# An mLSTM, GLA and SSD decoder trunk on one core: the mLSTM's row operations begin at the second GLA value, and other steps of the lanes are moved

## Chip, core and metric

One core of a Trainium2 chip runs the whole program in one launch. The metric is the device time of one execution in microseconds (us), given as the median of several runs. A profile is one further execution, recorded instruction by instruction. The engines are named as the profile names them: PE (TensorE, matrix products; PEld are its weight loads), DVE (VectorE), ACT (ScalarE), POOL (GpSimd) and SP (SyncE, which issues most transfers).

## What is computed

The reference is one step of a two-layer decoder trunk on 512 prompt tokens and 8 x 4 sample tokens, 544 tokens in all, with 1024 features, in 32-bit floats.

```python
def _trunk(x, ...):
    for l in range(DEPTH):
        if l % 2 == 0:
            mix, c, n, m, s = _ab_mixer(x, ...)
        else:
            mix, h, cv = _ssd_mixer(x, ...)
        x = _layernorm(DN_ALPHA * x + mix, ...)
        x = _layernorm(DN_ALPHA * x + _mlp(x, ...), ...)
```

The AB mixer of layer 0 has two groups of four heads, mLSTM and GLA, fed by one input projection, and one output projection behind both. The mLSTM's part that matters here is its row arithmetic, on one row of 544 numbers for each of four heads: a log-sigmoid, a running sum `b`, a running maximum, and exponentials of their differences.

```python
    lf = jax.nn.log_sigmoid(mf + fg_bias)
    b = jnp.cumsum(lf, axis=1)
    g = b + m0
    D = b[t] - b[s] + ig[s]          # for s <= t
    m = jnp.maximum(g, D.max(axis=2))
    w_intra, w_inter = jnp.exp(D - m), jnp.exp(g - m)
    h = num / jnp.maximum(jnp.abs(den), jnp.exp(-m))
```

GLA multiplies each score by the exponential of a difference of decays, feature by feature, which the kernel does level by level (1, 2, 4, ... 256 tokens). Layer 1 is a Mamba-2 SSD mixer. Behind each mixer stand a layer normalisation, a squared-ReLU MLP of 4096 features, and another normalisation.

## The kernel before

**Products.** Features lie on the 128 partitions and tokens in two halves of 272 columns. A 32-bit product is made of three products of rounded parts (hi by hi, hi by lo, lo by hi), so an output block of 128 features over 1024 input features is 8 x 3 = 24 matmuls for each half, 48 for both (`dense`, L378). This text calls one such matmul *a product*. Weights come by DMA; ACT makes the rounded part `whi` (L167) and DVE the rest `wlo` (L168).

**Order.** PE's order is written out by hand: within the AB, output projection, MLP and SSD stages PE runs exactly what the program lists, in that order. The order of DVE, ACT and POOL is not written out: a planner at compile time sorts their instructions by readiness and by the place at which they are listed. `issue_after` adds an edge: what is listed inside it stands behind a given instruction on that engine.

**Lanes.** All small work (scores, transposes, normalisations) is written as generators, the *lanes*. `tick()` is called ahead of every product and moves each lane by one; `yield n` lets n further ticks pass, so what follows stands n + 1 products later in PE's order. `W` (L36) holds those numbers by name. `need(key)` polls once a tick until another lane has set the key; it costs no instruction. `until` and `flush` drive lanes on without products.

**The AB stage** runs 20 blocks (GLA's q, k and v, the mLSTM's q, k and v, and GLA's gate gg), 960 products, then four tail blocks (the mLSTM's output gate mo), the first half of all four and then the second, 192 products. Between the halves, at product 1056, `until("mheads")` forces the mLSTM's heads to an end; `take_place` then closes the pool with the score tiles and lists four loads of the residual `xf` on POOL (L325). The lanes in it:

- `gla_lane`: `gla_decay` (steps `dec`), then for each of two feature blocks `gla_scores`: the diagonal `gd` after `s0` products for the first block and `sc` for the second; nine levels (`gs`), `lev` apart, each with a difference F on POOL (L1085), two exponentials on ACT (L1087, L1088), and zq and zk on DVE (L1092, L1094); then a transpose `kdt` after `kd`. Then the sample scores (`ss`), the final state (`end`), and `gla_samples` and `ml_samples`, each with `c0` ahead of its values, `u` ahead of each of six outer products `supd` (L1008, with a masked copy `vm` on POOL, L1004) and `s` ahead of the last transpose.
- `gla_heads`: for each head the value `num` (L869), on whose emission the key ("g", h) is set; its normalisation ends in four instructions on ACT that write `hn` (L897); `out` products later a transpose `hot` (L903), and after `hd` the next head. The keys ("gT", q) hold heads 0 and 1, then 2 and 3, back until the scores of block q are there.
- `ml_lane`: `ml_gates` lists the row arithmetic in three blocks, each inside `hold("head")`, which puts it behind the last DVE and ACT instruction of the GLA value listed last. The first block is L1226 to L1237, and stands behind `need("gscores")`, a key that `gla_lane` sets when the scores of both feature blocks are there; in the same tick, just before it, value 2 is listed. The second (L1241 to L1254) and third (from L1258) need ("g", 2). After ("g", 3), `gates` products on, PE transposes the rows (`uwt`, L1280), and `gr` and again `gr` later come small matmuls `sc` (L1288 to L1293). Then `pipeline` runs the four heads of the mLSTM in steps `mr` products apart, with up to four heads at different points in one step: transpose, scores (`md`, `mo`), value, and a broadcast row (`rowbc`). `ml`, a wait within a head's generator, has no effect there: `pipeline` takes no notice of it.
- `tokmajor` (lane "v", steps `v`): transposes of v.

PSUM tiles of this stage come from `pm`, which takes a fifth tile of its own on each fifth call and otherwise goes round four.

**Normalisations** (`layernorm`) are two steps per half, sum and variance: `l0` and `v0` for the first half, `l1` and `v1` for the second, `ls` and `vs` instead for the second half ahead of MLP 1. The last one (`last_layernorm`) has `f0`, `f1` and `f2`. In SSD, `sg` stands ahead of each group's first step.

Of the kernel before, what the change touches and what calls it, by code (L numbers as in the profile page):

```python
# [32 lines left out]
HEADM = 6  # L33
HEADA = 2

W = dict(dec=12, gates=30, gr=8, sc=16, lev=16, v=24, kd=10, out=48, hd=6, s0=42, ss=40, end=12, c0=20, u=13, s=16, ml=12, mr=52, dt=238, sg=72, sx=14, sq=26, so=48, l0=12, l1=12, v0=74, v1=55, f0=16, f1=18, f2=4, ls=20, vs=47)  # L36
GATES = ((0, 0, 4), (32, 4, 4), (64, 8, 16))
LEVELS = (64, 32, 16, 8, 4, 2, 1)

# [189 lines left out]
def trunk_kernel(ctx, tc, a, stages=("ab", "mlp0", "ssd", "mlp1")):  # L229
# [8 lines left out]
    def pm(name):  # L238
        turn[0] += 1
        k = spare[0] and turn[0] % 5 == 0  # L240
        return psm.tile([P, 512], F32, tag="k" if k else "m", name=name, bufs=1 if k else 4)
# [91 lines left out]
    def need(*keys):  # L333
        while not ready.issuperset(keys):
            yield 0
# [114 lines left out]
    def layernorm(hf, i, pool, out=None):  # L450
# [4 lines left out]
        which = norms_done[0] - hf  # L455
        yield W["l0" if not hf else "ls" if i == 2 else "l1"]
        mu = pm("mu")
# [8 lines left out]
        V.tensor_tensor(q[:, 0], q[:, 0], q[:, 1], ALU.add)  # L466
        yield W["v0" if not hf else "vs" if i == 2 else "v1"]
        var = pm("var")
# [34 lines left out]
    def last_layernorm(i, pool, out):  # L503
# [6 lines left out]
        def less(mu, k, f):  # L510
            V.scalar_tensor_tensor(x[:, k:k + 2], mu[:, None, :n].broadcast_to([P, 2, n]), f, x[:, k:k + 2], ALU.mult, ALU.add)
        yield W["f0"]
        mu = pm("mu")
# [9 lines left out]
        for k in range(h, KT - 1):  # L523
# [4 lines left out]
            V.tensor_tensor(q[:, 0], q[:, 0], q[:, k], ALU.add)  # L528
        yield W["f1"]
        mu, var, rp = pm("mu"), pm("var"), pm("rp")  # L530
        TE.matmul(mu[:, :n], ones, s, start=True, stop=False)
        yield W["f2"]
        TE.matmul(var[:, :n], ones, q[:, 0], start=True, stop=False)
# [182 lines left out]
    def ab(pool, early, then):  # L716
# [67 lines left out]
        def tokmajor(key, h):  # L784

            x = fm[key + "v", h]
            if h == 0:
                vt[key] = pool.tile([P, 4, 4, 130], F32, tag="vt", name="vt", bufs=2)
                G.memset(vt[key][:, :, :, 128:], 1.0)
                vraw[key] = pool.tile([P, 4, NS], F32, tag="vs", name="vs", bufs=1)  # L790
            yield W["v"]
            p = pm("vtr")
# [337 lines left out]
        def hold(what="last", mx=None):  # L1130

            st = ExitStack()
            for x in (mx or gla)[what]:
                st.enter_context(tc.issue_after(x))
            return st
# [79 lines left out]
        ml = {}  # L1215

        def ml_gates():
            rw = early.tile([P, T], F32, name="rw", bufs=1)
            uw = early.tile([P, T], F32, name="uw", bufs=1)
            z, t, b, u = rw[0:4], rw[32:36], rw[64:68], uw[0:4]  # L1220
            G.memset(uw, 0.0)
            S.copy(z, gate[32:36])
            S.copy(u, gate[0:4])
            yield from need("gscores")
            with hold("head"):
                S.activation(t, z, AF.Abs)  # L1226
                S.activation(t, t, AF.Exp, scale=-1.0)
# [173 lines left out]
        def ml_lane():  # L1401
            ml["cg"] = []
            yield from need(("gate", 0))
            yield from ml_gates()
            yield from need("gla", ("mq", 1), ("mk", 1))
            rows_bc(ml["nM"][:, :NP])
            ready.add("mscores")
            yield from pipeline([ml_head(h) for h in range(4)], W["mr"], (3, 1, 2, 0))
            ready.add("mheads")
            yield from ml_last()  # L1410
            ready.add("ml")
# [531 lines left out]
    while n < len(stages):  # L1943
        st = stages[n]
        src = spill
        with ExitStack() as stk:
            if st == "ssd":
# [5 lines left out]
                with tc.tile_pool(name="ssd", bufs=1, reuse_waits="tile") as pool:  # L1953
# [4 lines left out]
                    with tc.manual_schedule(engines={mybir.EngineType.PE}):  # L1958
                        out = ssd(pool, ypool, dram, right, ahead, consts)
# [174 lines left out]
```

## Time and profile before

| | us |
|---|---|
| median of 3 runs | 1504.7 |
| lowest and highest | 1504.12, 1508.48 |
| profiled execution, device time | 1502.27 |
| its span, first to last instruction | 1500.6 |

The prediction shows the profile's lines. In the page and the tables of stretches, each engine's busy time is in us, with the number of instructions behind x; PEclk is the clock granted to TensorE, as a share of full speed or, in the row of 40 digits, in tenths. A line of a timeline has the start in us from the first instruction, the duration, the engine, the line of the kernel, the operation, output <- inputs, sizes, the number of instructions merged, and in brackets the idle time of the engine ahead of it with what ended that. A matmul's duration is its latency; successive matmuls overlap, so it is their starts that show the rate.

### The profile page before, as it was taken

The numbers are of one execution on the slowest core, as the hardware profiler recorded it, in microseconds if no ns is written. First come the engines' busy times: TensorE is split into PE (matmuls) and PEld (weight loads), VectorE is DVE, ScalarE is ACT, GpSimd is POOL, SyncE is SP. The second block draws the span as 40 slices with busy tenths as digits, with TensorE's granted clock in tenths as the row PEclk, the third lists the DMA queues.
The fourth block names the chain that finished last, engine by engine and source line by source line (L and its number), as shares of the span: only waits on it lengthen the run. The fifth ranks groups of instructions, "written<-read, shape, count | busy, mean of one in ns | idle before, by whom it ended". The sixth has DMA issues, their size and how long they took to land.

```text
span 1500.6 us, 29204 instructions
## 1 busy us (share of the span) xinstructions
PE 1468.2 (98%) x11607; PEld 1419.1 (95%) x11607; DVE 1100.2 (73%) x2075; ACT 795.0 (53%) x1750; POOL 192.8 (13%) x228
## 2 busy tenths in 40 slices
PE   9998989999999999999999999999999999999997
PEld 8988989999999999999888789989999999999996
DVE  5675576786777667668999988777678677676656
ACT  7454457474444534537776675555247354444343
POOL 1410222100000000010243441421010000000000
PEclk9998999999999999999999999999999999999998
DMA  7211333413232332416657766365222333233221
GB/s 252 71 57 43 88 120 90 126 43 114 72 113 90 94 99 85 146 48 202 141 144 257 235 191 226 99 205 151 71 75 67 99 100 96 88 99 92 63 86 60
DMA packets 95025, 172.51 MB, mean 115 GB/s; under 512 B 15880, under 2 KB 50968, under 8 KB 94632
## 3 DMA queue, kind: packets, MB, share of 16 engines
q1 hardware_dynamic: 62280, 140.44, 30.3%
q10 hardware_dynamic: 29216, 17.19, 4.4%
q0 software_dynamic: 3392, 13.00, 2.3%
q8 instruction: 91, 1.49, 0.4%
q14 instruction: 46, 0.38, 0.1%
HBM read 153.48 MB, written 17.13 MB: 114 GB/s over the span
## 4 chain that ended last, share of the span: by engine, by line
PE 44%; DVE 5%; DMA 1%; issue 1%; ACT 1%; SPq 0%; DVEq 0%
PE psd L378 30%; PE psd L590 9%; PE yp L1712 1%; DVE wlo L168 1%; DVE acc L1606 1%; PE it L1759 1%; PE sp L1690 1%; PE ip L1687 1%; PE sps L1766 1%; DMA wraw<-mlp_w 0%; DVE h0n L1772 0%; PE xt L1651 0%; DMA ec<-d_ecs 0%; DVE xf L552 0%; DVE Y L1715 0%
## 5 line engine op out<-in xcount | busy, mean ns | idle before, releaser
L378 PE MATMUL psd<-xh,whi 128*128 128x272 f32 x1488 | 441.3, 297 | 1.0 <-ACT xh L287 1.0
L378 PE MATMUL psd<-xl,whi 128*128 128x272 f32 x1488 | 435.5, 293 | 1.3 <-DVE xl L478 1.3
L378 PE MATMUL psd<-xh,wlo 128*128 128x272 f32 x1488 | 435.7, 293 | 0.0
L378 PEld LDWEIGHTS psd<-xl,whi 128*128 128x128 f32 x1488 | 281.8, 190 | 7.9 <-issue 4.0
L378 PEld LDWEIGHTS psd<-xh,whi 128*128 128x128 f32 x1488 | 281.4, 189 | 8.0 <-issue 4.7
L378 PE MATMUL psd<-hh,whi 128*128 128x272 f32 x992 | 286.9, 289 | 0.0
L378 PE MATMUL psd<-hlo,whi 128*128 128x272 f32 x992 | 286.5, 289 | 0.0
L378 PE MATMUL psd<-hh,wlo 128*128 128x272 f32 x992 | 286.4, 289 | 0.0
L378 PEld LDWEIGHTS psd<-xh,wlo 128*128 128x128 f32 x1488 | 281.6, 189 | 4.4 <-issue 3.5
L168 DVE TENSOR_TENSOR wlo<-wraw,whi 128x1024 fp32r<-128x1024 f32 (+2 forms) x175 | 206.6, 1184 | 54.3 <-ACT whi L167 52.8
L167 ACT CAST whi<-wraw 128x1024 fp32r<-128x1024 f32 (+2 forms) x175 | 173.5, 997 | 130.2 <-PE psd L378 108.6
L378 PEld LDWEIGHTS psd<-hlo,whi 128*128 128x128 f32 x992 | 186.9, 188 | 0.2
L378 PEld LDWEIGHTS psd<-hh,whi 128*128 128x128 f32 x992 | 186.9, 188 | 0.2
L378 PEld LDWEIGHTS psd<-hh,wlo 128*128 128x128 f32 x992 | 186.9, 188 | 0.1
L428 DVE TENSOR_TENSOR xf<-xf,psd 128x272 f32<-128x272 f32 x208 | 88.4, 434 | 74.7 <-PE psd L378 74.2
L590 PE MATMUL psd<-xh,wlo 128*128 128x272 f32 x416 | 120.0, 289 | 0.0
L590 PE MATMUL psd<-xh,whi 128*128 128x272 f32 x416 | 119.9, 288 | 0.0
L590 PE MATMUL psd<-xl,whi 128*128 128x272 f32 x416 | 119.7, 288 | 0.0
L203 ACT CAST whi<-wsum 128x1024 fp32r<-128x1024 f32 x52 | 54.3, 1044 | 111.3 <-PE psd L590 70.2
L203 ACT CAST whi<-wraw 128x1024 fp32r<-128x1024 f32 (+1 forms) x52 | 43.4, 834 | 95.3 <-PE psd L378 84.2
L204 DVE TENSOR_TENSOR wlo<-wsum,whi 128x1024 fp32r<-128x1024 f32 x52 | 63.7, 1225 | 23.2 <-ACT whi L203 23.2
L590 PEld LDWEIGHTS psd<-xl,whi 128*128 128x128 f32 x416 | 78.5, 189 | 0.0
(488 smaller groups left out, 2836.4 us busy)
## 6 DMA issues: line engine op xcount, KB each, us to landing
wraw<-mlp_w SPq DMA_DIRECT2D x80, 512.0 KB, 3.7
wraw<-ssd_in SPq DMA_DIRECT2D x40, 512.0 KB, 3.8
wraw<-mlp_w SPq DMA_DIRECT2D x64, 256.0 KB, 3.0
wraw<-ab_in SPq DMA_DIRECT2D x22, 512.0 KB, 3.7
h<-h SPq DMA_DIRECT2D x32, 256.0 KB, 4.7
h0n<-h0n SPq DMA_DIRECT2D x16, 512.0 KB, 5.0
E<-d_cs ACTq DMA_DIRECT2D x16, 512.0 KB, 5.0
s_h<-h0n POOLq DMA_DIRECT2D x16, 512.0 KB, 4.0
```

Of the source, the lines that this page charges most:

```text
L167: nc.scalar.copy(hi[:, r], w[:, r])
L168: nc.vector.tensor_tensor(lo[:, r], w[:, r], hi[:, r].bitcast(F32), ALU.subtract)
L203: self.cut[0] = nc.scalar.copy(hi, x).ins
L204: self.cut[1] = nc.vector.tensor_tensor(lo, x, hi.bitcast(F32), ALU.subtract).ins
L378: last[0] = TE.matmul(ps[:, :TH], (hi, hi, lo)[t][:, k, :], (rh, rl, rh)[t], start=i == 0, stop=i == n - 1).ins
L428: V.tensor_tensor(x, x, ps, ALU.add)
L590: last[0] = TE.matmul(ps, wt[:, k], bt[:, k], start=first and n == 0, stop=n == 11, skip_group_check=not first).ins
L1606: V.scalar_tensor_tensor(acc[:, :n], ci[:, w:w + n], cw[:, m, w:w + 1], acc[:, :n], ALU.mult, ALU.add)
L1687: TE.matmul(ip[:, j * P:(j + 1) * P], hT[:, j * P:(j + 1) * P], Cf[:, tk], start=True, stop=True)
L1690: TE.matmul(sp, Bt[:, b], xw, start=True, stop=True)
L1712: TE.matmul(ypv[64 * e:64 * e + 64, j], z[:, 64 * r:64 * r + 64], E[:, r], start=True, stop=True)
L1759: TE.matmul(it[64 + NS * k:64 + NS * k + NS], Cm[:, NS * (q + k):NS * (q + k) + NS], h0[k], start=q == 0, stop=q == NB - 2)
```

## The change

The first block of the row arithmetic is held behind the key ("g", 1), the second GLA value (they are counted from 0), in place of "gscores". And 22 of the 31 numbers in `W` change: `mr` 52 to 62 (the mLSTM's heads), `s0` 42 to 36 (the first GLA level), and smaller moves of other lanes. No instruction is added or taken out.

```diff
-W = dict(dec=12, gates=30, gr=8, sc=16, lev=16, v=24, kd=10, out=48, hd=6, s0=42, ss=40, end=12, c0=20, u=13, s=16, ml=12, mr=52, dt=238, sg=72, sx=14, sq=26, so=48, l0=12, l1=12, v0=74, v1=55, f0=16, f1=18, f2=4, ls=20, vs=47)
+W = dict(dec=11, gates=30, gr=11, sc=18, lev=16, v=21, kd=12, out=48, hd=5, s0=36, ss=40, end=10, c0=18, u=14, s=14, ml=9, mr=62, dt=238, sg=71, sx=14, sq=26, so=48, l0=13, l1=14, v0=86, v1=60, f0=18, f1=18, f2=3, ls=27, vs=36)
...
             S.copy(z, gate[32:36])
             S.copy(u, gate[0:4])
-            yield from need("gscores")
+            yield from need(("g", 1))
             with hold("head"):
                 S.activation(t, z, AF.Abs)
```

## The prediction

> **What bounds the kernel now.** First the page: its first line and the granted clock of part 2.
>
> ```profile
> PE 1468.2 (98%) x11607; PEld 1419.1 (95%) x11607; DVE 1100.2 (73%) x2075; ACT 795.0 (53%) x1750; POOL 192.8 (13%) x228
> PEclk9998999999999999999999999999999999999998
> ```
>
> TensorE is the bound; a change pays only where PE idles or its clock drops (the 8 in the fourth slice). Next, busy time by stage (AB, output projection, MLP 0, SSD, the layernorm ahead of MLP 1, the end) and inside two stretches.
>
> ```profile
> core 0: us, PE busy (x) PEld busy (x) DVE busy (x) ACT busy (x) POOL busy (x), PEclk, DMA share, GB/s
> 0.00:254.40 254.40, 240.06 (x1880) 226.93 (x1881) 162.73 (x419) 138.71 (x324) 60.67 (x79) 0.97 0.34 103
> 254.40:303.60 49.20, 49.20 (x391) 49.04 (x390) 38.48 (x71) 23.23 (x42) 7.01 (x7) 1.00 0.37 120
> 1097.00:1130.00 33.00, 31.58 (x241) 30.64 (x241) 29.96 (x50) 21.17 (x40) 5.05 (x4) 1.00 0.28 85
> 131.00:146.00 15.00, 11.02 (x53) 10.10 (x52) 8.82 (x28) 6.76 (x17) 2.15 (x3) 0.66 0.10 37
> 219.00:228.00 9.00, 6.96 (x39) 6.27 (x38) 4.90 (x17) 4.39 (x12) 4.07 (x7) 0.81 0.72 267
> ```
>
> AB loses 14.3 us of PE and two spells of clock. A full-rate product costs 49.20/391 = 0.126 us. At half clock there were 1.0 - 0.66 = 0.34, over 0.5, of 15 us: 10.2 us; likewise 0.19/0.5 of 9 us: 3.4 us. Now PE's timeline, the rows in which it waited, and two products at half clock.
>
> ```profile
> 41.94 1.05 PE L1102 MATMUL gs<-zq,zk 128*128 128x128 f32 x8
> 95.17 1.13 PE L1102 MATMUL gs<-zq,zk 128*128 128x128 f32 x8 [1.96 <-DVE zk L1094]
> 134.21 0.87 PE L1280 MATMUL uwt<-con,uw 128*128 128x128 f32 x4 [3.04 <-ACT uw L1254]
> 135.10 0.43 PE L378 MATMUL psd<-xh,wlo 128*128 128x272 f32 x1
> 136.69 0.43 PE L378 MATMUL psd<-xh,whi 128*128 128x272 f32 x1
> 138.58 1.01 PE L1288 MATMUL sc<-ones,rw 4*128 4x2 f32 x4 [0.94 <-DVE rw L1271]
> 189.94 0.51 PE L769 MATMUL rowbc<-rb,selr 128*128 128x256 f32 x2 [1.36 <-DVE E L1322]
> 196.68 0.33 PE L1367 MATMUL mkt<-con,gkz 128*128 128x128 f32 x1 [1.55 <-ACT hn L897]
> 221.81 0.92 PE L1008 MATMUL supd<-vm,gkstk 128*128 128x390 f32 x2 [2.04 <-POOL vm L1004]
> ```
>
> From 135.10 to 136.69 are seven products: 0.227 us each, so half clock wastes 1 - 0.126/0.227 = 44% of its time. The two spells follow the waits of 3.04 and 2.04; after 1.96 there is none.
>
> **Positions.** Every lane ticks once a product, so a yield of W[x] moves a step x+1 products. Counted on PE's timeline (L378 rows ahead of the step), then by the new W, before to after: first GLA diagonal 202 to 193, first level 219 to 210; GLA value 0 366 to 359, second diagonal 383 to 378, value 1 422 to 414, value 2 547 to 544, value 3 603 to 599; uwt 634 to 630; mLSTM head steps 659, 712, 765, 818, 871, 924, 977 to 654, 717, 780, 843, 906, 969, 1032; the GLA samples' last outer product 800 to 802, the mLSTM's 956 to 965. The lane would end its heads at 1095, but the tails' drain at 1056 forces it; only the empty last gap is skipped.
>
> **Part 1, the row operations** (gain 8.1 us). The first block runs from L1226 to L1237, then the second ends in uwt's releaser.
>
> ```profile
> 92.15 1.50 ACT L897 ACTIVATE hn<-num,hb,hf 128x128 f32<-128x128 f32 x4 [0.82 <-DVE hb L894]
> 118.40 1.50 ACT L897 ACTIVATE hn<-num,hb,hf 128x128 f32<-128x128 f32 x4 [0.23 <-DVE hb L894]
> 119.93 0.66 ACT L1226 ACTIVATE rw<-rw 4x544 f32<-4x544 f32 x1
> 130.09 1.28 DVE L1237 TENSOR_TENSOR_SCAN rw<-rw 4x544 f32<-4x544 f32 x1
> 131.40 0.72 DVE L1241 TENSOR_TENSOR rw<-rw 4x544 f32<-4x544 f32 x1
> 133.50 0.66 ACT L1254 ACTIVATE uw<-uw 4x544 f32<-4x544 f32 x1 [0.70 <-DVE uw L1252]
> ```
>
> The block starts behind value 2's hn and takes until 131.4. With need(("g", 1)) it goes behind value 1's hn (93.7). The second block still waits for value 2 and takes 134.16 - 131.40 = 2.8 us: begun at 119.9 it ends near 123 to 125, while uwt, four products sooner, is due near 130. Gone: 3.04, then L1288's 0.94 (its rows follow the second block), then 44% of the 9.3 us that PE worked at half clock, 4.1. Cover: about 5 us; were it gone, as much of the 8.1 would return as the block is late. The gates' and gr steps' own shifts are part of these positions and cost nothing.
>
> The price (2.5 us). Ten instructions, three ACT of 0.66 (2.0 us) and seven DVE of some 5.0 us together (two scans of 1.28, two of 0.72, two of 0.43, one of 0.14), now stand between value 1 and the later GLA levels, where PE already waits 1.96 us for zk. ACT's queue there: the four hn, then exponentials of F for three levels; the block may go between them, and whatever of F, zk and the mask copies stands behind it on ACT and DVE then waits, with PE behind zk.
>
> ```profile
> 94.60 0.42 DVE L1094 TENSOR_TENSOR zk<-gk,F 128x256 f32<-128x256 f32 x1
> 95.54 1.27 DVE L1094 TENSOR_TENSOR zk<-gk,F 128x256 f32<-128x256 f32 x1
> 98.47 0.41 DVE L1094 TENSOR_TENSOR zk<-gk,F 128x256 f32<-128x256 f32 x1
> 95.17 1.37 POOL L1085 TENSOR_TENSOR F<-A 128x512 f32<-128x512 f32 x1 [8.89 <-DVE zk L1094]
> ```
>
> Bounds: 0 (it fits into DVE's holes) and 7.0 (all ahead of one level); zk is two levels ahead of PE soon after 98, so I take 2.5. The Trainium skill, GPSIMD Engine Reference, "1. Specifications", says that GpSimd shares its SBUF interface with VectorE and contends with its two-input instructions; by it the moved operations, beside POOL's F, would run longer. The rows agree: zk 1.27 beside F, 0.42 without. If each of three F lengthened a row operation by the same 0.85, the price would be 5.1 and the sum 2.6 us less, 1500.7; I keep 2.5, as only some overlap.
>
> **Part 2, heads 62 apart** (gain 5.5, price 0.8). POOL at the wait of 221.81, and DVE ahead of 189.94:
>
> ```profile
> 218.69 2.20 POOL L325 DMA_DIRECT2D xf<-xT  x4
> 220.90 1.42 POOL L1004 TENSOR_TENSOR vm<-vstk,con 128x390 f32<-128x390 f32 x2
> 189.09 0.17 DVE L965 COPY c<-n 128x8 f32<-128x8 f32 x1 [2.44 <-DMA s_S<-c]
> 179.13 0.66 PE L794 MATMUL vtr<-con,mv 128*128 128x128 f32 x4
> 171.28 2.40 PE L869 MATMUL num<-vt,E 128*128 128x130 f32 x20
> ```
>
> The four loads of xf need the space of E, free when the last head's value (924) is read, and stand ahead of vm. At 969 that value lies behind the last outer product (965), so vm goes first: 2.04, and 44% of the 3.4 us at half clock, 1.5: 3.5. The loads, some 5 us later, are needed at product 1176, 207 products (26 us) after 969. The copy L965 blocked DVE on a store; E's multiply, the release of rowbc's bank, and hn behind it were late: 1.36 and 1.55. The step is now 25 products (3.1 us) later and the store hardly, so the copy is through first; the next sample step follows 13 products after it, so I count 2.0 of 2.9 (bounds 0 and 2.9). Price: PSUM tiles of this stage go round five banks, so each waits for the fifth before it; hn freed that bank 7.9 us after num began (171.28 to 179.13). The tile that now waits for value 0 is the last GLA outer product, 22 products behind the step: 2.2 + 0.5 + 2.8 and two small tiles of 1.1 is 6.6 us. It may wait 1.2 (bounds 0 and 1.2); 0.8. Last transposes at 1032 leave 120 products (15 us) before the output projection.
>
> **Part 3, first level sooner** (price 0.8). Its step moves 9 products, 1.1 us; dec gives back only one.
>
> ```profile
> 40.05 1.25 DVE L1094 TENSOR_TENSOR zk<-gk,F 128x256 f32<-128x256 f32 x1
> ```
>
> zk ends at 41.30, PE starts at 41.94: 0.6 us of cover, so 0.5 late, and the next two levels, behind the same full DVE, somewhat more. Bounds 0 and 1.1.
>
> **Part 4, layernorms** (price 2.5) **and end** (0.4). v0 and l0 set the first half's variance 13 products, 1.6 us, later.
>
> ```profile
> 1108.89 0.50 DVE L481 SCALAR_TENSOR_TENSOR xf<-xf,lnp,lnr 128x272 f32<-128x272 f32 x1
> 1120.76 1.32 DVE L478 SCALAR_TENSOR_TENSOR xl<-xf,lnp,xh 128x272 fp32r<-128x272 f32 x3
> 1121.31 0.39 PE L378 MATMUL psd<-xl,whi 128*128 128x272 f32 x1 [1.28 <-DVE xl L478]
> 1122.08 0.62 PE L458 MATMUL mu<-lns,ones 128*128 128x272 f32 x2
> 1128.22 0.44 DVE L466 TENSOR_TENSOR lnq<-lnq 128x272 f32<-128x272 f32 x1
> 1489.25 0.73 PE L536 MATMUL mu<-xf,ones 128*128 128x272 f32 x2
> ```
>
> Ahead of MLP 1 DVE works without a gap from 1108.89 to the xl that PE waits for, so a later start is paid there: bounds 0.5 (conversions fill in) and 1.6, I take 1.2. ls and vs leave 37 products for mu's squares and sums: 0.62 + 37 x 0.126 = 5.3 us, where DVE needed 1128.66 - 1122.08 = 6.6; the variance waits 1.3 (bounds 0 and 1.3). The other two layernorms have no such wait; v1's five products lie under a first half of 144 products. f2 puts the variance pair ahead of the last product, whose eviction it covered until the row at 1489.25: 0.4 (0 to 0.6). The remaining shifts (c0, u, s, end, kd, hd, v, l1, f0, and sg by one product in SSD; ml has no effect) are a few tenths of a us of place, beside products: 0, with 0.5 either way.
>
> **Sum.** 8.1 + 3.5 + 2.0 - 2.5 - 0.8 - 0.8 - 2.5 - 0.4 = 6.6 us. The profiled execution took 1502.27 (span 1500.6 and 1.7 around it); it becomes 1495.7. The median of the runs shown, 1504.7, is 2.4 above it; on that scale **1498.1**.
>
> The Trainium skill, TensorE: Matmul & The Clock Gate, "Why this matters for your kernels", advises no PE gap over about 3 us, lest the clock drop. By it the gap of 2.04 would have had no spell behind it, and its removal be worth 1.5 less: 1499.6. The trace differs: 2.04 did halve it.
>
> **Rivals.** (a) *Cheaper*: the block fits into holes and the layernorms pay their lower bounds (0.5 and 0): 2.5 + 2.0 back and the 0.9 left of 2.9: 1492.7; chance 0.12. For it: DVE is 73% busy; against: it is full at 95. (b) *Half is eaten*: the lane sets only PE's order; the planner places DVE's, ACT's and POOL's own work, and may leave the loads ahead of vm or the copy where it is: 5.5 less, 1503.6, no measurable change; chance 0.30. For it: that order is not written in the code; against: each needs an event that moved. That the change does nothing, row operations staying late, is in this case: then 8.1 stays, but so does 2.5: 1503.7. (c) *Slower*: the block goes ahead of one level's F on ACT and zk on DVE, PE waits 1.96 + 7.0 there and its clock halves as after 3.04: 7.0 + 4.1 instead of 2.5, and 5.5 does not come: 1512.2. With the 5.5 missing (1503.6) the sign turns once 3.6 us are lost there, and from 8.1 it can be measured; chance 0.13. For it: ACT's queue at 92.15; against: zk's lead after 98. The forecast keeps 0.45.
>
> **Range.** 1491 to 1508 takes in (a), (b) and the bounds; some 2 in 10 lie outside. A measurement of this kernel tells about 0.3% (4.5 us) from no change. Faster, below 1500.2: 0.45 + 0.12 = 0.57; within: 0.30; slower: 0.13.
>
> **What would show it.** L1226 near 94 instead of 119.93, uwt without a wait, a 9 in the fourth slice of the clock; L325 behind the last vm; rowbc and mkt unhindered. Prices: larger waits of gs near 95, new ones at gs near 41, at the third supd of the GLA samples, at var near 1128, and over 1.28 near 1121. Wrong would be a gs wait with half clock behind it, or L1226 unmoved.

## Result and the profile after

The changed kernel takes 1487.24 us in the median (1486.99 to 1487.69, 4 runs), the kernel before 1504.41 beside it (1499.3 to 1508.48, 4 runs): a ratio of 0.9888, 95% interval 0.9857 to 0.9918. The two profiled executions, 1487.29 and 1502.27, lie 15.0 us apart. The forecast was 6.6 us: the sign is right, the size is not, and 1487.2 is below the range.

First the page of the changed kernel: engines, and the granted clock in 40 slices.

```profile
PE 1461.6 (98%) x11607; PEld 1414.2 (95%) x11607; DVE 1095.2 (74%) x2075; ACT 792.0 (53%) x1750; POOL 187.8 (13%) x228
PEclk9999999999999999999999999999999999999998
```

The 8 in the fourth slice is gone. Busy time by stretches of the changed kernel follows: AB, output projection, the layernorm ahead of MLP 1, and the two places that had lost clock (AB now ends near 235.7 instead of 254.4).

```profile
0.00:235.70 235.70, 232.99 (x1880) 221.97 (x1881) 160.15 (x419) 136.35 (x323) 60.87 (x79) 1.00 0.36 110
235.70:284.90 49.20, 49.20 (x391) 49.04 (x390) 37.73 (x70) 23.40 (x43) 5.44 (x7) 1.00 0.40 122
1080.00:1115.00 35.00, 31.54 (x241) 30.63 (x240) 30.46 (x51) 22.23 (x42) 5.37 (x4) 1.00 0.25 80
110.00:131.00 21.00, 21.00 (x176) 20.85 (x174) 15.79 (x60) 12.50 (x34) 2.04 (x2) 1.00 0.22 64
198.00:207.00 9.00, 9.00 (x65) 8.33 (x64) 6.19 (x19) 6.91 (x19) 3.58 (x5) 1.00 0.44 122
```

AB, with the same 1880 matmuls, loses 235.70 - 232.99 = 2.7 us of PE instead of 14.3, and no clock at all. Its last waits, and those of the layernorm, are these rows of PE's timeline:

```profile
91.48 1.13 PE L1102 MATMUL gs<-zq,zk 128*128 128x128 f32 x8 [0.77 <-DVE zk L1094]
107.59 1.98 PE L1115 MATMUL gs<-zq,zk 128*128 128x512 f32 x4 [0.23 <-DVE zq L1092]
1103.78 0.39 PE L378 MATMUL psd<-xl,whi 128*128 128x272 f32 x1 [0.95 <-DVE xl L478]
1105.47 0.62 PE L458 MATMUL mu<-lns,ones 128*128 128x272 f32 x2
1112.87 0.70 PE L469 MATMUL var<-lnq,ones 128*128 128x272 f32 x2 [2.15 <-DVE lnq L466]
```

Waits of uwt, sc, rowbc, mkt and supd no longer stand there; those of gs fell from 2.69 (0.73 and 1.96) to 1.00; the variance has a new one. The start of every product can be compared between two profiled runs. How far the changed kernel is ahead at some of them gives the gain by stage, beside what the forecast's terms come to there:

| stage (products counted from the start) | forecast, us | measured, us |
|---|---|---|
| GLA levels and values (to 630) | -0.8 - 2.5 = -3.3 | +2.1 |
| uwt, sc and the half clock behind them (to 660) | +8.1 | +8.8 |
| heads and sample steps (to 1152, the end of AB) | 5.5 - 0.8 = +4.7 | +7.8 |
| projection, MLP 0, SSD (to 6936) | 0 | -1.2 |
| layernorm ahead of MLP 1 (to 7300) | -2.5 | -2.1 |
| the end | -0.4 | -0.4 |
| sum | +6.6 | +15.0 |

Of the 8.4 us missed, 5.4 lie ahead of product 630 and 3.1 in the heads and sample steps. The experiments look there.

### The profile page after: what moved, and what is told of

Same layout as the page of the kernel before. It is cut to its first block, busy times and chain, and to the rows that moved or that the text cites. A ratio compares the mean times of both kernels' runs of the same rounds, so it can differ in the third digit from the quotient of the medians.

```text
span 1485.6 us, 29194 instructions
## 1 busy us (share of the span) xinstructions
PE 1461.6 (98%) x11607; PEld 1414.2 (95%) x11607; DVE 1095.2 (74%) x2075; ACT 792.0 (53%) x1750; POOL 187.8 (13%) x228
## 5 line engine op out<-in xcount | busy, mean ns | idle before, releaser
L378 PE MATMUL psd<-xh,whi 128*128 128x272 f32 x1488 | 433.1, 291 | 0.6 <-ACT xh L287 0.6
L167 ACT CAST whi<-wraw 128x1024 fp32r<-128x1024 f32 (+2 forms) x175 | 173.3, 996 | 134.0 <-PE psd L378 119.2
L590 PE MATMUL psd<-xh,whi 128*128 128x272 f32 x416 | 119.8, 288 | 0.0
```

Of the source, the lines that this page charges most:

```text
L167: nc.scalar.copy(hi[:, r], w[:, r])
L378: last[0] = TE.matmul(ps[:, :TH], (hi, hi, lo)[t][:, k, :], (rh, rl, rh)[t], start=i == 0, stop=i == n - 1).ins
L590: last[0] = TE.matmul(ps, wt[:, k], bt[:, k], start=first and n == 0, stop=n == 11, skip_group_check=not first).ins
```

## Experiments

"Theory" and its letter are those of the expectations. R stands for the row arithmetic's early first block, G for the GLA numbers s0, sc, dec, kd, hd, M for mr = 62. "Ahead at AB's end" is how much sooner than in the kernel before (254.44 us) the first product behind AB starts, in the profiled runs; waits and half clock are those of AB, in us, summed from PE's timeline and the clock's record. sc is counted with uwt; "other" are further waits of the sample steps. The half clock, and with it the lead at AB's end, is partly chance (last section): a spell of 3.4 us more or less is 1.5 us at AB's end, so the medians stand beside.

| kernel | median us | ratio to before, 95% | ahead at AB's end | gs | uwt | rowbc, mkt | supd | other | half clock |
|---|---|---|---|---|---|---|---|---|---|
| before | | 1 | 0 | 2.69 | 3.98 | 2.91 | 2.29 | 0 | 13.7 |
| e1: R | 1494.61 | 0.9925 (0.9908-0.9943) | 9.2 | 3.53 | 0 | 0.34 | 2.30 | 0 | 6.8 |
| e10: G | 1495.37 | 0.9952 (0.9934-0.9969) | 10.0 | 0.27 | 4.04 | 0 | 1.39 | 1.45 | 3.4 |
| e6: M | 1501.41 | 0.9979 (0.9963-0.9994) | 0.9 | 2.71 | 4.74 | 0 | 2.72 | 0.67 | 17.1 |
| e9: R, M | 1496.82 | 0.9952 (0.9938-0.9966) | 6.5 | 4.96 | 0 | 0 | 2.72 | 1.87 | 3.4 |
| e11: R, G | 1488.48 | 0.9896 (0.9875-0.9918) | 16.1 | 1.05 | 0 | 0 | 1.39 | 0.42 | 0 |
| e13: R, G, M | 1484.67 | 0.9871 (0.9849-0.9894) | 18.0 | 1.04 | 0 | 0 | 0 | 0.39 | 0 |
| after | 1487.24 | 0.9888 (0.9857-0.9918) | 18.7 | 1.00 | 0 | 0 | 0 | 0 | 0 |
| e2: after without R | 1491.03 | 0.9914 (0.9889-0.9938) | 11.6 | 0 | 4.12 | 0 | 0 | 0 | 10.2 |
| e3: after without M | 1491.55 | 0.9906 (0.9889-0.9924) | 12.8 | 1.00 | 0 | 1.94 | 1.03 | 0.87 | 3.4 |
| e5: hd 4 | 1496.51 | 0.9942 (0.9923-0.9961) | 6.1 | 1.67 | 3.86 | 1.40 | 1.21 | 0 | 10.2 |

### The early block alone (e1)

The kernel before with one edit:

```diff
-            yield from need("gscores")
+            yield from need(("g", 1))
```

> The kernel before with one edit alone: the row arithmetic's first block behind ("g", 1), all numbers of W as before. Theory A (the block's early start is worth its forecast 8.1 us by itself and costs nothing among the GLA levels): uwt's wait of 3.04, sc's of 0.94 and the half-clock spell near 135 go, the gs waits stay near 2.7 us in all, and the profiled run takes some 1494 (1502.3 - 8.1). Theory B (the block has its price of 2.5 and other numbers of the change hide it): the same gone, but the gs waits grow to about 5 us, 1496 to 1497. Theory C (the wait for uwt went since the GLA lane as a whole stands earlier, not since the block does): uwt still waits 2 us or more, 1500 to 1503.

Measured: 1494.61, profiled 1494.45. uwt and sc wait for nothing. PE's timeline at the later GLA level, and the stretch around it:

```profile
95.56 1.13 PE L1102 MATMUL gs<-zq,zk 128*128 128x128 f32 x8 [2.78 <-DVE zk L1094]
```

```profile
90.00:102.00 12.00, 9.22 (x64) 9.03 (x64) 9.07 (x12) 8.92 (x26) 3.60 (x3) 0.86 0.16 45
```

The wait of 1.96 grew to 2.78, and the clock averages 0.86 over 12 us, so it was halved for (1 - 0.86) x 12 / 0.5 = 3.4 us. From product 400 to 550 this run falls 2.5 us behind before's pace: the price of 2.5 was right for this edit by itself, though it is 0.8 of wait and the rest clock (theory B in kind, A in its time). From 630 to 660 it gains 8.5. What no theory had: mkt's and rowbc's waits shrank from 2.91 to 0.34 with mr still 52. On DVE the copy L965, which the forecast holds to have delayed them, waits for nothing here (2.44 before):

```profile
179.61 0.17 DVE L965 COPY c<-n 128x8 f32<-128x8 f32 x1
```

### The early block undone (e2)

The changed kernel with the key "gscores" again:

```diff
-            yield from need(("g", 1))
+            yield from need("gscores")
```

> The changed kernel with the first block behind "gscores" again, the new W kept. Theories A and B: uwt waits again (it is four products sooner than before, the block not: 3 us or more), sc too, and a half-clock spell may follow: by A 1487.3 + 8 = 1495, by B 1487.3 + 8 - 2.5 = 1493. Theory C: uwt waits little, 1487 to 1489.

Measured: 1491.03. PE's timeline has uwt's wait back:

```profile
130.12 0.66 PE L1280 MATMUL uwt<-con,uw 128*128 128x128 f32 x4 [3.23 <-ACT uw L1254]
```

and 10.2 us of half clock behind it: theory C, that the lane as a whole came earlier, falls. gs waits for nothing in this run, so within the new numbers the block's price is the 1.00 us that the changed kernel still waits there. Put in, the block gains 18.7 - 11.6 = 7.1 at AB's end. By the medians 3.8 of it is left: up to the end of SSD e2 gains 1.4 where the changed kernel gives back 1.2, and its layernorm ahead of MLP 1 costs 0.7 less.

### The GLA numbers alone (e10)

```diff
-dec=12, sc=16, kd=10, hd=6, s0=42
+dec=11, sc=18, kd=12, hd=5, s0=36
```

> The kernel before with the GLA lane's numbers alone: s0 36, sc 18, dec 11, kd 12, hd 5 (levels and values some eight products sooner, first level nine). Theory K (these numbers cost nothing at the first level and take the gs waits of 2.7 away, which part 3 had priced at 0.8 the other way): no wait at gs near 41, gs waits in all under 0.3 near 80 and 93, 2.5 us gained at product 550; uwt's wait, sc's and the half clock behind them stay. Theory L (part 3 as forecast): 0.5 to 1.1 lost at the first levels and the gs waits of 2.7 kept.

Measured: 1495.37, 10.0 ahead at AB's end, some 3 of it by chance (the spell behind uwt was 3.4 us long here, 10.2 in before); 3.5 us ahead of before at product 550, of which 0.3 were there at product 100. Only 0.27 of the gs waits is left and the first level has none: theory K. Why the first level costs nothing is seen in the changed kernel, which has the same numbers. First, DVE's timeline before:

```profile
33.65 1.28 DVE L1043 TENSOR_TENSOR_SCAN A<-con,lat 128x544 f32<-128x544 f32 x1
38.01 2.12 DVE L1043 TENSOR_TENSOR_SCAN A<-con,lat 128x544 f32<-128x544 f32 x1
```

and after, with the zk of the first level:

```profile
30.85 1.29 DVE L1043 TENSOR_TENSOR_SCAN A<-con,lat 128x544 f32<-128x544 f32 x1
35.62 1.26 DVE L1094 TENSOR_TENSOR zk<-gk,F 128x256 f32<-128x256 f32 x1
40.17 1.28 DVE L1043 TENSOR_TENSOR_SCAN A<-con,lat 128x544 f32<-128x544 f32 x1
```

When the PE step moved by 1.1 us, the planner put the first feature block's scan 2.8 us sooner and its zk ahead of the second block's scan (40.17), which before had stood ahead of zk (38.01, with zk at 40.05). zk now ends at 36.9, with PE's first level at 40.5. DVE's chain, which part 3 held rigid, was sorted anew. Supd waits 1.39 instead of 2.04 here. No number of the sample steps had changed, but the lanes hang together: the mLSTM's head steps stand five products sooner (the last value at 919 instead of 924), its last outer product six later (962 instead of 956). And the copy L965 still holds DVE up, for 3.05 us; the 1.03 of sho among the other waits comes right behind it.

### Values 1 and 3 two products sooner (e5)

```diff
-hd=6
+hd=4
```

> The kernel before with hd = 4 instead of 6 alone: values 1 and 3 of GLA stand two products (0.25 us) sooner, no GLA level moves. In the planner's order this is enough for value 1's second hf (L880) and its hb (L894) to stand ahead of a weight block's cast whi and rest wlo instead of behind them. Theory G1 (the gs wait of 1.96 was value 1's hn, late behind whi and wlo, with the exponentials of F behind it on ACT; it went in the changed kernel since value 1 stands sooner): the wait at gs near 95 falls to 0.5 or less, 1502.3 - 1.5 to 2 = 1500.5. Theory G2 (it went since the levels themselves stand sooner): it stays near 1.9, 1502 to 1503. Either way uwt's wait, sc's and the half-clock spells stay.

Measured: 1496.51. ACT's timeline in the kernel before, around value 1's hn:

```profile
89.36 0.30 ACT L879 ACTIVATE hf<-bmv,epsc 128x4 f32<-128x4 f32 x1 [5.47 <-DVE bmv L874]
89.74 1.05 ACT L167 CAST whi<-wraw 128x1024 fp32r<-128x1024 f32 x1
90.69 0.20 ACT L880 ACTIVATE hf<-hf 128x4 f32<-128x4 f32 x1
...
92.15 1.50 ACT L897 ACTIVATE hn<-num,hb,hf 128x128 f32<-128x128 f32 x4 [0.82 <-DVE hb L894]
93.54 0.42 ACT L1087 ACTIVATE F<-F 128x256 f32<-128x256 f32 x1
```

and in this run:

```profile
89.14 0.30 ACT L879 ACTIVATE hf<-bmv,epsc 128x4 f32<-128x4 f32 x1 [5.23 <-DVE bmv L874]
89.47 0.21 ACT L880 ACTIVATE hf<-hf 128x4 f32<-128x4 f32 x1
89.77 1.05 ACT L167 CAST whi<-wraw 128x1024 fp32r<-128x1024 f32 x1
...
91.16 1.52 ACT L897 ACTIVATE hn<-num,hb,hf 128x128 f32<-128x128 f32 x4
92.54 0.45 ACT L1087 ACTIVATE F<-F 128x256 f32<-128x256 f32 x1
```

Before, a weight block's cast stands between the two small hf of value 1; hn waits for them, and on ACT the exponentials of F stand behind hn. A quarter of a microsecond on PE swaps cast and hf, F starts 1.00 us sooner (93.54 to 92.54), and the gs wait falls from 1.96 to 0.94, by 1.02: theory G1's mechanism, with 1.0 of the 1.5 to 2 us that it named. In the changed kernel value 1 is eight products sooner; ACT's timeline there:

```profile
87.64 1.51 ACT L897 ACTIVATE hn<-num,hb,hf 128x128 f32<-128x128 f32 x4
89.18 0.66 ACT L1226 ACTIVATE rw<-rw 4x544 f32<-4x544 f32 x1
89.86 0.42 ACT L1087 ACTIVATE F<-F 128x256 f32<-128x256 f32 x1
...
90.49 1.03 ACT L167 CAST whi<-wraw 128x1024 fp32r<-128x1024 f32 x1
...
92.45 0.66 ACT L1227 ACTIVATE rw<-rw 4x544 f32<-4x544 f32 x1
```

hn starts 4.5 us sooner than before (87.64 to 92.15), the cast stands behind it, and the row operations go one by one between the exponentials of F. Back in e5, supd's last wait of 2.04 and its spell are gone as well, though no number of those steps was changed: the two hd that stand ahead of them put the mLSTM's head steps four products sooner (last value 920) and leave its outer products where they were. That the run is 4 us faster than theory G1 had it comes from these steps, where it gains 4.9 us between products 661 and 965; which of the shifts does it was not separated.

### Early block and GLA numbers (e11)

R and G in the kernel before:

```diff
-dec=12, sc=16, kd=10, hd=6, s0=42
+dec=11, sc=18, kd=12, hd=5, s0=36
...
-            yield from need("gscores")
+            yield from need(("g", 1))
```

> The kernel before with the early first block and the same GLA numbers. Theory K, added up: gs waits of 1.0 (as in the changed kernel), no uwt, no sc, no half clock there: 9.2 + 2.5 + 1.5 = 13.2 gained at the end of AB if supd's 2.05 and its spell stay as with the early block alone; 1489 to 1491. If supd's wait goes too, 16 to 17, and 62 has nothing left to give; the changed kernel with 52 (12.8 at the end of AB) speaks against that.

Measured: 1488.48, 16.1 ahead at AB's end; gs waits of 1.05 as theory K has them, and supd with 1.39 and no spell. Alone, R gave 9.2 and G 10.0, together 16.1. At product 550 this run is 1.6 us behind G alone (e10): the block's price with the GLA numbers, after 2.5 without them.

### Heads 62 apart alone (e6)

```diff
-mr=52
+mr=62
```

> The kernel before with mr = 62 alone. Theory A as forecast (part 2 is worth 5.5 by itself less 0.8): supd's 2.04 goes, L325 stands behind the last vm, the spell at 223 goes, and rowbc and mkt wait under 1 us together: 1502.3 - 4.7 = 1497.6. Theory H (rowbc's and mkt's waits hang on when the row arithmetic and the samples' copies are through, not on the heads' distance; the run with the early block alone lost most of them): these 2.9 stay, supd and its spell go, 1502.3 - 3.5 = 1498.8. The gs waits of 2.7, uwt and sc stay by both.

Measured: 1501.41; 0.9 ahead at AB's end with one spell of 3.4 us more than before, and 3.2 by the ratio (0.9 to 5.6). POOL's timeline in this run at the mLSTM samples' outer products:

```profile
206.32 0.77 POOL L917 TENSOR_TENSOR cg<-cg,gg 128x272 f32<-128x272 f32 x1 [1.82 <-DVE gg L826]
214.26 0.70 POOL L917 TENSOR_TENSOR cg<-cg,gg 128x240 f32<-128x240 f32 x1 [7.18 <-DVE hf L890]
214.92 2.21 POOL L1004 TENSOR_TENSOR vm<-vstk,con 128x390 f32<-128x390 f32 x3
```

As part 2 says, the loads L325 no longer stand ahead of vm. But a multiply by the gate does (cg, L917): POOL idles 7.18 us until DVE is ready for it, and supd waits 2.72 for vm instead of 2.04, with half clock behind it. A new waiter took the old one's place: the rival "half is eaten". rowbc's and mkt's waits did go, but num has 0.67 and sc 1.69 instead of 0.94. Nor is the copy L965 through first, as part 2 had it. DVE idles longer for it than before (2.44):

```profile
187.67 0.18 DVE L965 COPY c<-n 128x8 f32<-128x8 f32 x1 [3.34 <-DMA s_S<-c]
```

The heads' distance only moves PE's steps away from what stands behind that copy.

### Early block and heads 62 apart (e9)

R and M in the kernel before:

```diff
-mr=52
+mr=62
...
-            yield from need("gscores")
+            yield from need(("g", 1))
```

> The kernel before with two edits: the early first block and mr = 62. Product by product up to the end of AB the early block alone gave 9.2 us against before, mr alone 0.9, and the changed kernel 18.7. Theory I (the parts add): 10.1 at the end of AB, gs waits of 3.5 and supd's of 2 to 2.7 stay, some 1492 to 1494. Theory J (62 pays only once the rows are early, since POOL's and DVE's queues at the last sample steps are in order then): supd 2.05 goes as well, 9.2 + 2.4 + 1.5 of half clock = 13 at the end of AB, 1490 to 1491.

Measured: 1496.82, 6.5 ahead: 2.7 less than the block alone, and 2.2 less by the medians. supd waits 2.72 behind the same cg, and the block shows its price in a row of PE's timeline, where the DVE instruction that ended the wait is one of the row operations:

```profile
110.03 0.67 PE L1102 MATMUL gs<-zq,zk 128*128 128x256 f32 x2 [1.45 <-DVE rw L1234]
```

From product 400 to 550 this run falls 2.5 us behind before's pace, as e1 does: there with 0.8 of wait and a spell, here with 0.8 and 1.45 of wait and no spell, so the price of the block by itself does not hang on the clock. Both theories fall: with the old GLA numbers the parts do not even add.

### All three (e13)

R, G and M in the kernel before; the numbers of samples, gates, v and layernorms as before:

```diff
-dec=12, sc=16, kd=10, hd=6, s0=42, mr=52
+dec=11, sc=18, kd=12, hd=5, s0=36, mr=62
...
-            yield from need("gscores")
+            yield from need(("g", 1))
```

> The kernel before with three edits: the early first block, the five GLA numbers (s0, sc, dec, kd, hd) and mr = 62; samples', gates', v and layernorm numbers as before. Without mr this gave 16.1 us at the end of AB with supd's 1.39 and vtr's 0.42 left; mr without the GLA numbers gave 6.5. Theory N (62 pays, but only on top of the GLA numbers, since these bring POOL's gate products and the samples' copies of vm into the order of the changed kernel): supd and vtr wait for nothing, gs waits of 0.8 to 1.2 stay, 18 to 18.7 gained at the end of AB and, with the layernorm numbers of before, 1484 to 1487. Theory O (the small numbers of the samples, c0 18, u 14, s 14, end 10, or gr and v, put that order right): supd or mkt still waits 1 or more, 13 to 16.5 gained at the end of AB.

Measured: 1484.67, 18.0 ahead at AB's end, supd and vtr without a wait. POOL's timeline shows the order that the changed kernel has too:

```profile
193.50 0.84 POOL L1004 TENSOR_TENSOR vm<-vstk,con 128x390 f32<-128x390 f32 x1
195.21 0.84 POOL L1004 TENSOR_TENSOR vm<-vstk,con 128x390 f32<-128x390 f32 x1 [0.87 <-PE mo L1328]
199.65 1.17 POOL L1004 TENSOR_TENSOR vm<-vstk,con 128x260 f32<-128x260 f32 x1 [3.60 <-PE supd L1008]
202.29 0.71 POOL L917 TENSOR_TENSOR cg<-cg,gg 128x240 f32<-128x240 f32 x1 [1.48 <-DVE gg L826]
206.03 0.77 POOL L917 TENSOR_TENSOR cg<-cg,gg 128x272 f32<-128x272 f32 x1 [3.02 <-DVE gg L826]
206.73 1.14 POOL L325 DMA_DIRECT2D xf<-xT  x2
```

The last vm stands ahead of the next products by the gate (cg), and the loads behind these: theory N. 62 apart is worth 0.9 alone, -2.7 with R, +1.9 with R and G at AB's end; 3.2 by the ratio, -2.2 and +3.8 by the medians. The other numbers of AB (gr, v, end, c0, u, s) add 0.8 at AB's end.

### Heads 52 apart in the changed kernel (e3)

```diff
-mr=62
+mr=52
```

> The changed kernel with the mLSTM heads 52 products apart again (mr alone). Theory A (the 62 alone removed the waits of rowbc, mkt and supd): rowbc and mkt wait 2.9 us again, supd 2.0 with L325 ahead of the last vm, with 1.5 to 2 of half clock behind it: 1487.3 + 4.9 to 6.9 = 1492 to 1494. Theory D (those waits went since the row arithmetic was through sooner, or since the lanes of the samples moved): no such wait, 1487 to 1488.5.

Measured: 1491.55; mkt waits 1.94, supd 1.03, vtr 0.87, and half clock of 3.4 us follows mkt: 18.7 - 12.8 = 6.0 (unrounded) lost at AB's end, 4.3 by the medians. Theory A in its time, though not row by row (rowbc waits for nothing, supd for half): in this company 62 is worth about what part 2 forecast, which the runs of it alone and with R do not tell.

### The layernorm numbers (e4, e7) and the changed kernel again (e8)

e4 takes all six back, in the changed kernel:

```diff
-l0=13, l1=14, v0=86, v1=60, ls=27, vs=36
+l0=12, l1=12, v0=74, v1=55, ls=20, vs=47
```

e7 the last two:

```diff
-ls=27, vs=36
+ls=20, vs=47
```

and e8 none: it is the changed kernel itself.

> The changed kernel with the layernorm numbers of before (l0 12, l1 12, v0 74, v1 55, ls 20, vs 47). Theory E (the 2.2 us that the changed kernel loses ahead of MLP 1 come from these numbers): var's wait of 2.15 goes, xl's stays near 1.3, 1487.3 - 2.2 = 1485.1. Theory F (the loss comes from the SSD stage ending in another state, with DVE later there): the wait stays or moves to xl, 1487.0 to 1487.5.

> The changed kernel with ls 20 and vs 47 as before, the other layernorm numbers new. Theory E1 (the wait of 2.15 for the variance ahead of MLP 1 hangs on these two, the 37 products that they leave for mu's squares and sums being too few): var waits 0 to 0.3, and 1487.24 - 2.0 = 1485.2; SSD's first transpose xt keeps its short wait of 0.2 (it had 2.23 with all layernorm numbers old). Theory E2 (v0 and l0, the first half's variance 13 products later, cause it): a wait of 1 to 2 stays at var, 1486 to 1487.2.

> The changed kernel once more, unaltered, on the chip and in the hour of the three others: 1487.2 within 0.5, to compare the run with ls and vs of before against. Its lowest and highest should lie within 1 us, those of the kernel before some 5 apart, if the half-clock spells are what scatters the latter's times.

Measured: 1485.21 (e4), 1483.66 (e7; 1482.32 to 1484.15) and 1486.47 (e8; 1485.51 to 1488.66); e7 to before 0.9857 (0.9840 to 0.9873). PE's timeline in e7 has mu and var without a wait:

```profile
1103.48 0.62 PE L458 MATMUL mu<-lns,ones 128*128 128x272 f32 x2
...
1110.20 0.70 PE L469 MATMUL var<-lnq,ones 128*128 128x272 f32 x2
```

From mu to var are 1110.20 - 1103.48 = 6.7 us and 48 products; the changed kernel left 37 and waited 2.15. Theory E1: ls and vs cost all of it. v0 and l0, which e7 keeps, gain 0.3 us in the first half and lose it again in the second. e4, with those old too, has the wait of 2.23 at SSD's first transpose that the kernel before has. e7 beats both kernels. e8's median lies 0.8 us below the first one, and its times spread over 3.2 us, not 1 as expected; its granted clock goes from 0.997 for the fastest to 0.995 for the slowest.

### The block held behind a level (e12)

e7 with the first block held 75 products later, behind the GLA level listed last there (`hold()` takes that level's instructions):

```diff
             yield from need(("g", 1))
-            with hold("head"):
+            yield 75
+            with hold():
```

> The changed kernel with ls 20 and vs 47 (1483.66), and the first block held not behind value 1 but, 75 products later, behind the second feature block's level then listed last, so that the exponentials of F for four levels stand ahead of it on ACT. Theory M (the gs waits of 0.77 and 0.23 are the price of the block among the levels, and the second block leaves room): both go, uwt still does not wait, 1483.66 - 1.0 = 1482.6. Rival: the block ends later than value 2's hn, the second block with it, and uwt waits 1 or more, with half clock behind it above 2: 1484 to 1488.

Measured: 1483.80 (1482.86 to 1484.62), no difference from e7. uwt still waits for nothing and the wait of 0.77 is gone, but one of 0.71 stands at the last level (0.23 before): a price moved along the queue, 0.3 us less in all.

## Why the forecast was wrong

**Part 1, 8.1 gained: right.** 8.8 in the changed kernel, 8.5 with the block alone; uwt, sc and 10.2 us of half clock come back together when it is undone. L1226 stands behind value 1's hn as forecast, at 89.18 and not near 94, since hn itself came sooner; and the planner did not put the block in one piece.

**Part 1, price 2.5: right for that edit by itself, wrong beside the others.** The 2.5 was picked between bounds of 0 and 7, so that it fits to a tenth is luck. e1 shows 2.5 at that place, e11 against e10 1.6, and e2 beside the changed kernel 1.0 of wait.

**The step that failed** is the sentence of part 4 that the remaining shifts, kd and hd among them, "are a few tenths of a us of place, beside products: 0, with 0.5 either way", with part 3's price of 0.8 for s0. Positions were counted on PE's order alone, and DVE's and ACT's orders were taken to move along unchanged. GLA's values and levels, up to nine products sooner, were to cost 0.8; alone they gain about 3 us ahead of product 550 (e10). Of such gains, hd = 4 alone gives 1.0, since value 1's hf goes ahead of a weight cast (e5); at the first level the 0.8 does not fall due, since a scan goes behind zk. This and the smaller price of the block make up the 5.4 us ahead of product 630. The profile had the rows for it: in the kernel before, the cast L167 begins 0.08 us behind the first hf (L879) and keeps the second (L880) waiting, so that a shift of a quarter microsecond decides which goes first.

**Part 2, 4.7: the sum was near, the reason was not.** 62 was priced as if it alone put vm ahead of the loads. It did (e6), and the next instruction in POOL's queue, cg, took the loads' place. The waits of rowbc and mkt, put down to the copy L965 and the heads' distance, went nearly whole with the early block alone (e1) and whole with the GLA numbers (e10); in the changed kernel mkt's comes back, with 1.94, when 62 is undone there (e3). "The copy is through first" does not hold: with 62 it keeps DVE idle for 3.34 us (e6), and the changed kernel's 0.55 belongs to the whole change:

```profile
175.62 0.17 DVE L965 COPY c<-n 128x8 f32<-128x8 f32 x1 [0.55 <-DMA s_S<-c]
```

The price of 0.8 for the outer product that waits for value 0 is nowhere seen. In the changed kernel this stage gains 7.8: all of PE's 5.2 us of waits, the 1.5 of the spell, and 1.1 that no wait shows. Which order on DVE and POOL each of the numbers sets here stays open.

**Part 4: the sum of 2.5 was near (2.1), its split was not.** All is ls and vs (2.15 of wait against 1.3 forecast): DVE's last sum for the variance ends 7.25 us behind mu's start and not 6.58, since in the changed kernel DVE takes up mu behind a conversion (hlo) for which it idles:

```profile
1106.51 0.44 DVE L288 TENSOR_TENSOR hlo<-hr,hh 128x272 fp32r<-128x272 f32 x1 [1.96 <-ACT hh L287]
```

v0's later start was hidden. The end, 0.4, was right.

**Not forecast:** from AB's end to the end of SSD the changed kernel gives back 1.2 us. From product 4400 to 4500, around the layernorm ahead of SSD, it loses 0.8 and e4 and e13, with the old layernorm numbers, nothing; these two wait 2.2 at SSD's first transpose instead, where the changed kernel waits 0.2. The rest is not the kernel's alone: in e8, the same kernel profiled again, these stages gain 0.6.

**Scale.** Between medians the gain is 17.2, between profiled runs 15.0: before's profiled run was one of its faster ones. In 40 runs of the kernel before in these comparisons the time goes from 1499.60 at a mean granted clock of 0.995 to 1508.13 at 0.989: by the forecast's reckoning, 0.006 of clock is 0.006 x 1504 / 0.5 = 18 us at half clock, and 44% of that 7.9 of the 8.5 us between them. So before's spread is its clock, and the changed kernel has fewer waits that can halve it.

**Rivals.** (a), cheaper, named the right direction (1492.7), with 5.5 us too little; the block's price did fall to 1.0, but the layernorms cost nearly what was forecast. (b) came true for the part it was about, in the kernel with that part alone. (c) has its beginning in e1 and e9 (gs waits of 2.78 with half clock behind one of them), but not the sign.

## What to carry to other kernels

Where PE's order is written by hand and a planner sorts the other engines, a step moved by a few products is priced by what it is swapped with on ACT, DVE and POOL: look for rows that stand within some tenths of a microsecond of a cast or a load in the same queue, and take small shifts there as worth a microsecond either way. Do not sum such parts: 62 was worth 0.9, -2.7, +1.9 and +6.0 us at AB's end depending on its company, so undo each edit in the finished kernel as well as doing it alone. A wait that goes near 2 us may be worth its clock too.

## What the runs showed of the hardware

The same wait, SSD's first transpose with DVE's ncs ahead of it, in the kernel before and in e1. First before, PE's timeline and then the stretch around it:

```profile
736.08 0.63 PE L1651 MATMUL xt<-scon,Y 128*128 128x128 f32 x4 [2.22 <-DVE ncs L1567]
```

```profile
733.00:743.00 10.00, 7.78 (x60) 6.92 (x59) 9.27 (x18) 8.72 (x28) 4.43 (x7) 1.00 0.82 145
```

and the two views of e1:

```profile
727.12 0.63 PE L1651 MATMUL xt<-scon,Y 128*128 128x128 f32 x4 [2.23 <-DVE ncs L1567]
```

```profile
724.00:734.00 10.00, 7.77 (x49) 6.84 (x47) 9.27 (x18) 8.72 (x28) 3.79 (x6) 0.83 0.70 148
```

2.22 us left the clock at 1.00; 2.23 us halved it for (1 - 0.83) x 10 / 0.5 = 3.4 us. Over all profiled runs, 10 of 18 PE waits from 1.8 to 2.3 us were followed by a halved clock, 9 of 10 from 2.5 us up, and of single waits from 0.9 to 1.7 us that began at full clock none.

Where the clock changes tells what the chance is. The spells in AB and SSD last 3.4, 10.2 or 13.7 us: one, three or four times 3.413. The stretches of full clock between them are whole multiples of it too (in the kernel before 129.71 = 38 x 3.413 and 78.51 = 23 x 3.413), so within a run the changes lie on one grid. Its first full interval begins at 3.96 to 6.66 us, differently from run to run. In these intervals of the grid PE was busy as follows. In the kernel before, they are those of the waits of 1.96, 2.04 and 2.22:

```profile
93.55:96.96 3.41, 1.79 (x15) 1.82 (x16) 2.97 (x5) 2.33 (x9) 1.37 (x2) 1.00 0.35 138
219.84:223.25 3.41, 1.44 (x8) 1.17 (x9) 2.05 (x6) 1.88 (x7) 2.47 (x4) 1.00 0.91 317
731.84:735.25 3.41, 2.02 (x19) 1.74 (x17) 3.41 (x6) 1.10 (x3) 1.67 (x2) 1.00 1.40 166
```

and in e1 that of the wait of 2.23:

```profile
724.75:728.17 3.42, 1.19 (x11) 1.08 (x10) 3.42 (x11) 2.51 (x9) 2.13 (x5) 1.00 1.13 196
```

PE was idle for 1.62, 1.97, 1.39 and 2.23 us of them; behind the second and the fourth the clock is halved. So it is in all 15 profiled runs between 20 and 1465 us: of the intervals at full clock, all 22 with 1.73 us or more of idle PE are followed by half clock, and none with 1.72 or less is. A wait of 2.2 us halves the clock when it falls into one interval, and does not when the grid's edge splits it; even one of 2.78 in e9 did not, split into 1.69 and 1.09. Three times two waits of 0.85 to 1.21 us fell into one interval and together did. An estimate from these figures: a wait of 2.0 us has 1.73 of it in one interval for (2.0 - 2 x 1.73 + 3.41) / 3.41 = 0.57 of the grid's positions, beside the 10 of 18 seen. So the forecast's reading that 2.04 halves and 1.96 does not was chance, since the grid cut 0.34 us off the 1.96 and 0.07 off the 2.04, and 1.5 us for such a spell is the price of what may or may not come.

The Trainium skill, TensorE: Matmul & The Clock Gate, "What's actually happening", says that the gate judges activity over a window of 3413 ns which runs freely, regardless of the kernel. The grid agrees with that. The same page's advice in "Why this matters for your kernels", no gaps over about 3 us, does not hold here, since waits of 1.8 to 2.3 us sufficed in 10 of 18 cases.
